# Seven products for w2: 18 of the 22 activation blocks of both FFNs go through nine block pairs, with their activation sums made earlier and kept in DRAM

## The chip, the cores and the metric

The kernel runs on one core of a Trainium2 chip. The time is the device time of one execution in microseconds, as the median of several runs. A profiled execution is a run of its own with its own time; its trace gives the span from the first to the last instruction.

The engines named below: PE is TensorE (matmuls; it writes to PSUM), DVE is VectorE, ACT is ScalarE, POOL is GpSimd, and SP is SyncE, whose queue issues nearly all DMAs in order. "L673" is line 673 of the kernel before; lines of the changed kernel are marked as such.

## The reference

One step of a decoder trunk for 1024 prompt and 32 sample positions, 1056 columns in all, with a model width of 1024. Two FFNs (half steps) enclose a mixer of attention and gated MLP. All is float32:

```python
def swiglu(x, w1, w3, w2):
    return (jax.nn.silu(x @ w1) * (x @ w3)) @ w2          # 1024 -> 2816 -> 1024
...
    h = layer_norm(ALPHA * x + 0.5 * swiglu(x, f1_w1, f1_w3, f1_w2), ln1_g, ln1_b)
    z = h @ w_in + b_in
    ...                                                    # attention, gated MLP: mix
    h = layer_norm(ALPHA * h + mix, ln2_g, ln2_b)
    h = layer_norm(ALPHA * h + 0.5 * swiglu(h, f2_w1, f2_w3, f2_w2), ln3_g, ln3_b)
```

## The kernel before

**Layout.** Activations lie transposed: 128 features on the partitions, the 1056 columns along the free dimension, cut into four chunks of 264 (C). The inner width of an FFN, 2816, is 22 blocks of 128 (f = 0 to 21); the outer width, 1024, is 8 blocks.

**Precision.** Each float32 operand is split into a high and a low part: ACT casts the high part (L213), DVE subtracts it for the low part (L214). A product of 128x128 by 128x264 is then three matmuls, high by high, high by low and low by high (mm3, L202).

**w1 and w3.** For f = 1 to 21, w1 and w3 are one product of 2x2 blocks, done in seven products after Strassen and Winograd rather than eight (hidden). The sums of the activations are made once per FFN (spread, L291 and L301), those of the weights for each f (prep): POOL adds and subtracts (L337 and on), ACT and DVE split. One f takes 7 x 24 = 168 matmuls. Partial products are copied out of PSUM by ACT into buffers M, of which there are six (L397, L399, L400), and joined by DVE (L398, L401, L404, L406, L408). The hidden block, 128x1056, is stored to DRAM (L409).

**w2.** The 22 hidden blocks come back in groups of 2, 4, 6, 6 and 4 (GROUP2). Each loaded block (L614) is split on ACT and DVE. For each of the 8 output blocks and 4 chunks, a group is 3 matmuls per hidden block into one PSUM bank, and DVE adds the bank to the running output Y (L673, the eviction). Nothing here goes by seven products. The last group runs chunk by chunk, with centring (L437 to L448), squares (L487, L491) and normalisation (L497 to L526) of the layer norm between its blocks, and in the first FFN the splits of the next projection's first weights. The sums over columns that the mean needs come from L622 and L624.

**What sets the order.** Generators hold background work in queues (bg, slow, mid); each block ends with a tick that moves them by the number of steps in STEPS or MID. A scheduler then orders each engine's instructions by priority; evictions are urgent. PSUM has three banks tagged mm and five tagged ax. A DMA on SP's queue also waits for the one eight before it. Buffers: 37 slots S of 4 KB (and a little) per partition, eight W for split weights, two R for raw ones, two Q, six M.

## Time and profile before

| | us |
|---|---|
| median of 3 runs | 2258.15 (2256.51 to 2259.08) |
| the profiled execution | 2261.7 |
| its span | 2259.9 |
| first FFN, w1/w3 stage | about 53 to 474 |
| first FFN, w2 stage | 474 to 730 |
| projection, mixer | 730 to 1545 |
| second FFN, w1/w3 stage | 1545 to 1985 |
| second FFN, w2 stage and tail | 1990 to 2260 |

Stages overlap by a few microseconds. Busy time is read for each stage apart, with the engine's share of that stage's length; for PE a missing share is time in which it waited, and the waits name the engine and line that ended them. Some matmul records are missing from a trace, so that counts of a window are a little low.

### The profile page before, as it was taken

How to read it: one execution, taken by the hardware profiler on the slowest of the kernel's cores; microseconds unless marked ns; L12 is line 12 of the kernel's file. 1: busy time of each engine (PE TensorE's matmuls, PEld its weight loads, DVE VectorE, ACT ScalarE, POOL GpSimd, SP SyncE). 2: the span in 40 equal slices, each digit the busy share in tenths (PEclk: the TensorE clock that was granted, in tenths of full speed). 3: DMA queues.
4: the chain of work that ended last, by engine and by line, in shares of the span. 5: the costliest groups of instructions: out<-in, count | busy, mean ns of one | idle time of the engine just before them, and what ended most of it. 6: DMA issues, size and time to landing. Idle time of an engine off the chain costs nothing.

```text
span 2259.9 us, 42304 instructions
## 1 busy us (share of the span) xinstructions
PE 2225.1 (98%) x18031; PEld 2178.4 (96%) x18031; DVE 1185.6 (52%) x2026; ACT 812.2 (36%) x1489; POOL 244.1 (11%) x209
## 2 busy tenths in 40 slices
PE   8999999999999999999999999999999999999997
PEld 7999999999999988888999999999999999999997
DVE  8544344455448417557772624587443344365556
ACT  5333333321114554454463113256333333321114
POOL 3321222000000000000000000012322222000000
PEclk9999999999999999999999999999999999999998
DMA  4222233366324225444532312423332323544311
GB/s 153 95 95 104 95 106 112 123 211 199 134 83 133 108 78 169 126 154 152 182 103 80 108 46 77 175 77 126 120 104 95 113 104 107 208 132 156 100 38 78
DMA packets 81260, 268.61 MB, mean 119 GB/s; under 512 B 15968, under 2 KB 24912, under 8 KB 78384
## 3 DMA queue, kind: packets, MB, share of 16 engines
q1 hardware_dynamic: 80928, 265.86, 35.1%
q8 instruction: 141, 2.31, 0.4%
q14 instruction: 47, 0.39, 0.1%
q10 hardware_dynamic: 144, 0.05, 0.0%
HBM read 224.87 MB, written 87.20 MB: 138 GB/s over the span
## 4 chain that ended last, share of the span: by engine, by line
PE 87%; DVE 5%; DMA 3%; ACT 2%; issue 1%; POOL 0%; SPq 0%; DVEq 0%; ACTq 0%; POOLq 0%
PE mm L202 65%; PE ax L202 19%; DMA S<-kv 1%; PE ax L908 1%; PE ax L933 1%; PE ax L924 1%; DVE X L1087 1%; DVE S L1082 1%; DVE W L214 1%; DMA S<-cD 1%; ACT S L526 1%; DVE S L291 0%; DVE S L214 0%; DMA R<-w13a 0%; DMA S<-xc 0%
## 5 line engine op out<-in xcount | busy, mean ns | idle before, releaser
L202 PE MATMUL mm<-S,W 128*128 128x264 f32 x11040 | 1494.0, 286 | 7.4 <-ACT S L213 3.7
L202 PEld LDWEIGHTS mm<-S,W 128*128 128x128 f32 x11040 | 1401.3, 189 | 23.0 <-issue 7.7
L202 PE MATMUL mm<-S,S 128*128 128x264 f32 x2472 | 388.4, 285 | 5.0 <-POOL Q L337 2.6
L202 PE MATMUL ax<-S,W 128*128 128x264 f32 x2016 | 349.6, 284 | 0.0
L213 ACT CAST W<-R 128x1024 fp32r<-128x1024 f32 (+3 forms) x149 | 145.3, 975 | 553.7 <-PE mm L202 397.1
L202 PEld LDWEIGHTS mm<-S,S 128*128 128x128 f32 x2472 | 336.9, 189 | 6.2 <-POOL Q L337 2.7
L202 PEld LDWEIGHTS ax<-S,W 128*128 128x128 f32 x2016 | 288.1, 188 | 0.0
L202 PE MATMUL ax<-S,S 128*128 128x264 f32 x1512 | 266.0, 286 | 4.3 <-ACT S L213 4.3
L673 DVE SCALAR_TENSOR_TENSOR S<-mm,S 128x264 f32<-128x264 f32 x320 | 135.7, 430 | 198.0 <-PE mm L202 197.2
L214 DVE TENSOR_TENSOR W<-R,W 128x1024 fp32r<-128x1024 f32 (+3 forms) x149 | 169.2, 1136 | 117.8 <-ACT W L213 117.8
L202 PEld LDWEIGHTS ax<-S,S 128*128 128x128 f32 x1512 | 217.8, 189 | 4.7 <-ACT S L213 4.7
L401 DVE TENSOR_TENSOR S<-mm,M 128x264 f32<-128x264 f32 x42 | 18.2, 432 | 247.7 <-PE mm L202 242.8
L337 POOL TENSOR_TENSOR Q<-R 128x512 f32<-128x512 f32 x42 | 60.9, 1450 | 613.7 <-DMA R<-w13b 237.9
L81 POOL CAST S<-ones 128x1 fp32r<-128x1 f32 x32 | 10.1, 343 | 1008.7 <-PE mm L202 937.2
L213 ACT CAST S<-Q 128x1056 fp32r<-128x1056 f32 (+1 forms) x86 | 91.0, 1062 | 48.5 <-DMA Q<-hidA 21.8
L398 DVE TENSOR_TENSOR M<-M,mm 128x264 f32<-128x264 f32 x42 | 18.0, 428 | 169.5 <-PE mm L202 160.2
L214 DVE TENSOR_TENSOR S<-Q,S 128x1056 fp32r<-128x1056 f32 (+1 forms) x86 | 106.0, 1233 | 0.0
L405 ACT ACTIVATE S<-S 128x528 f32<-128x528 f32 x84 | 49.8, 638 | 83.8 <-DVE S L404 83.8
L397 ACT COPY M<-mm 128x264 f32<-128x264 f32 x42 | 15.9, 379 | 157.7 <-PE mm L202 157.7
L811 ACT ACTIVATE S<-mm,cols 128x264 f32<-128x264 f32 (+5 forms) x104 | 46.6, 492 | 65.0 <-PE mm L202 64.8
L912 ACT ACTIVATE M<-M,X 128x128 f32<-128x128 f32 (+1 forms) x96 | 42.7, 446 | 51.4 <-DVE X L909 51.0
L338 POOL TENSOR_TENSOR Q<-Q,R 128x512 f32<-128x512 f32 x42 | 60.1, 1430 | 2.7
(191 smaller groups left out, 1664.8 us busy)
## 6 DMA issues: line engine op xcount, KB each, us to landing
ws<-st SPq DMA_DIRECT2D x144, 256.0 KB
S<-kv SPq DMA_DIRECT2D x48, 512.0 KB
R<-w13b SPq DMA_DIRECT2D x44, 512.0 KB
R<-w13a SPq DMA_DIRECT2D x42, 512.0 KB
R<-wz SPq DMA_DIRECT2D x26, 512.0 KB
Q<-hidA SPq DMA_DIRECT2D x22, 528.0 KB
Q<-hidB SPq DMA_DIRECT2D x22, 528.0 KB
hidA<-S SPq DMA_DIRECT2D x21, 528.0 KB
```

The source lines that it names most:

```text
L202: mm = lambda a, b, s, e: nc.tensor.matmul(o, a[:, cc], b, start=s, stop=e, skip_group_check=True)
L213: self.nc.scalar.copy(hi, src)
L214: self.nc.vector.tensor_tensor(lo, src, hi.bitcast(F32), op=ALU.subtract)
L337: tt(s12[:, lo], cd[:, lo], cd[:, hi], op=ALU.add)
L338: tt(s12[:, hi], s12[:, lo], ab[:, lo], op=ALU.subtract)
L405: lambda x: nc.scalar.activation(h[:, x], h[:, x], AF.Silu),
L526: nc.scalar.activation(y[:, m], y[:, m], AF.Identity, bias=b, scale=g)
L673: nc.vector.scalar_tensor_tensor(y, po, HALF, y, op0=ALU.mult, op1=ALU.add)
L811: put = lambda o, x: nc.scalar.activation(o, x, AF.Identity, bias=b, scale=sc)
L908: nc.tensor.matmul(pS, q[e, i * P : (i + 1) * P], k[e, k0 : k0 + nk], start=True, stop=True)
L912: nc.scalar.activation(s[:, h, :nk], s[:, h, :nk], AF.Exp, bias=ml[:, 0, h, i : i + 1], scale=-1.0, accum_out=ml[:, 1, h, i : i + 1],)
L924: nc.tensor.transpose(pT[:, h, o], s[:, h, o], self.ident)
```

## The change

In both FFNs the hidden blocks 1 to 18 are taken as nine pairs. A pair of hidden blocks (rows), by two chunk pairs (columns), against a pair of output blocks is a 2x2 product of blocks, and it is done by seven products. Blocks 0, 19, 20 and 21 stay plain, 12 matmuls a block and chunk, and come last.

- **Activation sums.** After each even f the w1/w3 stage starts spill_sums for its pair as background work: four differences on DVE, and seven combinations split into high (ACT cast) and low (DVE). The 14 parts of 264 KB are stored to DRAM instead of two hidden blocks of 528 KB. The differences and the high parts use the six buffers M. Hidden blocks are only stored where they are plain.
- **Weight sums.** prep now serves w2 too, at 768 columns: three pairs against one output pair. There its sums are made on DVE, not on POOL; it runs 12 times per FFN.
- **The products.** The nine pairs go in three groups of three. seven does a group against one output pair: 7 products, two chunk pairs each, 9 matmuls for each of these, 126 in all, with an eviction into Y after every product and chunk pair (after: L759). This is done 12 times per FFN.
- **Loads.** 63 loads of 528 KB per FFN bring the sums back, already split (after: L717). For the first group they start in the last f of w1/w3 as its slots come free, mixed with the residual Y (after: L722); for the others they start one output pair before.
- **The end.** Centring starts with the plain blocks and not before them. Its partial means are gathered during the last products (gather). For the first chunk centring and squares come after its sixth block.
- **Others.** The bank pairs of hidden are arranged anew (banks), so two of its three pairs are one kind; MID is 3; the attention tables wait longer between steps.

The diff, cut:

```diff
-GROUP2 = ((2, 4), (4, 2), (6, 1), (6, 1), (4, 2))
+SEVEN = 9
+GP = 3
+NG = SEVEN // GP
+HP = GP * P
+ORDER = (1, 2, 6, 7, 5, 4, 3)
+PLAIN = (0, 19, 20, 21)
+NPL = len(PLAIN)
+NW = 2
+HEAD = 7 * GP + 2 * NC
+AHEAD = 4
...
-STEPS = dict(lead=6, strassen=3, out=2, project=2, gate=1, wout=3)
+STEPS = dict(lead=6, strassen=3, seven=2, out=2, project=2, gate=1, wout=3)
 PAUSE = 6
 REST = 3
-MID = 2
+GAP = 4
+LATE = 16
+MID = 3
...
-    def prep(self, w13, f):
-
-        nc, H = self.nc, KH * P
-        lo, hi = slice(0, H), slice(H, D)
+    def prep(self, src, f, H, engine):
+
+        nc = self.nc
...
-        tt = nc.gpsimd.tensor_tensor
+        tt = engine.tensor_tensor
...
+        else:
+            p4 = []
+            for h, l, w in ((ah, al, D - n), (h12, l12, H - (D - n))):
+                o = H + len(p4) * P
+                self.split(h[:, n : n + w], l[:, n : n + w], cd[:, o : o + w])
+                p4 += part(h, l, n)[: w // P]
...
+    def banks(self):
+        mm, ax = lambda: self.mm_tile()[:, :C], lambda: self.ax_tile()[:, :C]
+        return (ax(), ax()), (mm(), mm()), (mm(), ax())
+
     def hidden(self, f, between):
 
         nc = self.nc
-        bank = lambda: (self.mm_tile()[:, :C], self.ax_tile()[:, :C])
-        one, two, three = bank(), bank(), bank()
+        one, two, three = self.banks()
...
-        nc.sync.dma_start(self.hid[f], h.rearrange("p j h t -> p (j h t)"))
+        if f in PLAIN:
+            nc.sync.dma_start(self.hid[PLAIN.index(f)], h.rearrange("p j h t -> p (j h t)"))
+        elif f % 2:
+            self.odd = h
+        else:
+            self.bg.append(self.spill_sums(f // 2 - 1, self.odd, h))
+
+    def spill_sums(self, i, a, b):
+
+        nc = self.nc
+        x11, x12, x21, x22 = a[:, :, 0], a[:, :, 1], b[:, :, 0], b[:, :, 1]
+
+        def out(p, t):
+            hi = self.M([P, 2, C], F32R)
+            self.split(hi, t.bitcast(F32R), t)
+            dst = self.sums[i, ORDER.index(p)]
+            nc.sync.dma_start(dst[:, 0], hi.bitcast(F32))
+            nc.sync.dma_start(dst[:, 1], t)
+            return self.pause(GAP)
+
+        sub = lambda t, u, v: nc.vector.tensor_tensor(t, u, v, op=ALU.subtract)
+        t1, t2 = (self.M([P, 2, C]) for _ in range(2))
+        sub(t1, x12, x11)
+        yield from out(1, x11)
+        sub(t2, x22, t1)
+        yield from out(5, t1)
+        sub(x12, x22, x12)
+        yield from out(7, x12)
+        t4 = self.M([P, 2, C])
+        sub(t4, x21, t2)
+        yield from out(6, t2)
+        yield from out(3, x22)
+        yield from out(4, t4)
+        yield from out(2, x21)
...
+    def gather(self, c, i, m):
+
+        y = self.Y[c]
+        new = y[i // 2][:, 2 * (i % 2) : 2 * (i % 2) + 2]
+        if i == 1:
+            m = self.M([P, 2, C])
+        if i:
+            self.nc.vector.tensor_tensor(m, y[0][:, :2] if i == 1 else m, new, op=ALU.add)
+        return m
...
+                preps[f] = self.prep(w13[f], f, KH * P, nc.gpsimd)
+            else:
+                preps[f] = self.prep(w2p[f - FB], f, HP, nc.vector)
...
+            if f == FB - 1:
+                load(2)
+            count = iter(range(1, 8))
+
+            def after():
+                between(f, STEPS["strassen"])
+                if f == FB - 1:
+                    load(min(HEAD, 2 + 4 * next(count)))
...
+        self.U = [{p: [] for p in ORDER} for _ in range(NG)]
+        self.Y = [[None, None] for _ in range(NC)]
+        dma = self.nc.sync.dma_start
+
+        def sums(g, p, k):
+            t = self.S([P, 2, 2, C], F32R)
+            dma(t.bitcast(F32), self.sums[g * GP + k, ORDER.index(p)])
+            self.U[g][p].append(t)
+
+        def res(c, k):
+            self.Y[c][k] = self.S([P, KH, C])
+            dma(self.Y[c][k], resid[c, k])
+
+        first = {1: (0, 2), 7: (1, 3)}
+        for g in range(NG):
+            for p in ORDER:
+                for k in range(GP):
+                    yield lambda g=g, p=p, k=k: sums(g, p, k)
+                if g == 0:
+                    for c in first.get(p, ()):
+                        yield lambda c=c: res(c, 0)
+            if g == 0:
+                for c in range(NC):
+                    yield lambda c=c: res(c, 1)
...
+    def seven(self, f, g, np, between):
+
+        nc = self.nc
+        one, two, three = self.banks()
+        y = lambda x, r, e: self.Y[2 * x + e][(2 * np + r) // KH][:, (2 * np + r) % KH]
+        then = {
+            1: (one, 0, 0), 2: (two, 0, 0), 6: (one, 1, 0), 7: (three, 1, 1), 5: (one, 1, 1), 4: (three, 1, 0),
+            3: (one, 0, 1),
+        }
+        for p in ORDER:
+            bank, r, e = then[p]
+            for x in range(2):
+                for k in range(GP):
+                    u = self.U[g][p][k]
+                    self.mm3(
+                        bank[x], *self.L[f][p][k], u[:, 0, x], u[:, 1, x], p in (1, 2, 7) and k == 0, k == GP - 1
+                    )
+                with self.urgent():
+                    nc.vector.scalar_tensor_tensor(
+                        y(x, r, e), bank[x], HALF, y(x, r, e), op0=ALU.mult, op1=ALU.add
+                    )
+            between(p)
...
+                def step(p):
+                    k = ORDER.index(p)
+                    between(f, STEPS["seven"])
+                    if np == KB // 2 - 1:
+                        load(base + min(7 * GP, AHEAD + GP * (k + 1)))
+                    if g == NG - 1 and np == KB // 2 - 2 and k > 4:
+                        fetch(k - 5)
+                    if final:
+                        fetch(k + 2)
+                        if k in (1, 3):
+                            W2.append(next(self.w2units))
+                    if g == NG - 1 and np and 2 <= k < 2 + NC:
+                        means[k - 2] = self.gather(k - 2, np - 1, means[k - 2])
+
+                base = HEAD + 7 * GP * g
+                if np == KB // 2 - 2:
+                    load(base + AHEAD)
+                self.seven(f, g, np, step)
+                del self.L[f]
+                f += 1
...
+        for c in range(NC):
+            self.mid.append(self.center(c, hs, 3 if c else 5, means[c]))
+        centers = list(self.mid)[-NC:]
...
+            for k in range(NPL):
+                hi, lo = H[k]
+                self.mm3(po, w, k * NW * P + n % NW * P, hi[:, cc], lo[:, cc], k == 0, k == NPL - 1)
...
+            early = 6 if c == 0 else 0
+            if mode != "out":
+                self.hold_normed(c)
+                if c == 2:
+                    self.early = [self.unit(self.a["wz"][n], slot=True) for n in range(3)]
+                    self.early = self.early, [self.held([P, NT]) for _ in range(3)]
+            for n in range(KB):
+                if n == early:
+                    self.drain(centers[c])
+                    for m in range(early):
+                        self.square_step(c, m)
+                if c == 0 and n in (1, 3):
+                    W2.append(next(self.w2units))
+                block(n, c)
...
+        w = w2[1 : 1 + 2 * SEVEN].reshape(NG, GP, 2, P, KB // 2, 2, P).transpose(0, 4, 5, 3, 2, 1, 6)
+        A[f"w2p{s}"] = w[:, :, ::-1].reshape(NG * KB // 2, 2, P, 2 * HP)
```

How the instructions lie now, at three places. The names are tile names: M, S, W, R, Q are the buffers above, mm and ax PSUM banks, the numbers running.

ACT in the w1/w3 stage of the first FFN, before, with what each instruction waits for (DMAHW is a DMA lane, the loads and stores of SP's queue):

```order
L397 COPY M_3161<-ax_3156 128x264 [waits PE_49]
L213 CAST W_3375<-R_3369 128x1024 [waits DMAHW0_49,PE_49]
L399 COPY M_3162<-mm_3155 128x264 [waits PE_49]
L399 COPY M_3162<-ax_3156 128x264 [waits PE_49]
L400 COPY M_3163<-mm_3159 128x264 [waits PE_49]
L400 COPY M_3163<-ax_3160 128x264 [waits PE_49]
```

The same place of the changed kernel:

```order
L419 COPY M_3360<-ax_3354 128x264 [waits DMAHW7_49,PE_49,Activation_49]
L419 COPY M_3360<-ax_3355 128x264 [waits PE_49]
L224 CAST M_3396<-S_2875 128x528 [waits DMAHW2_49,Activation_49]
L224 CAST W_3610<-R_3604 128x1024 [waits DMAHW4_49,PE_49]
L224 CAST M_3434<-M_3393 128x528 [waits DVE_49,Activation_49]
L421 COPY M_3361<-ax_3354 128x264 [waits PE_49]
L421 COPY M_3361<-ax_3355 128x264 [waits PE_49]
L224 CAST M_3470<-S_2875 128x528 [waits DMAHW0_49,DVE_49,Activation_49]
L422 COPY M_3362<-mm_3358 128x264 [waits DMAHW2_49,DVE_49,PE_49]
```

Three casts of the sums now lie between the copies out of PSUM, and the first copy into a buffer M also waits for a DMA lane, that is for a store out of that buffer.

SP at the entry into the first FFN's w2 stage, before (L232 the residual, L614 hidden blocks):

```order
L232 DMA S_4963<-xc 128x1056
L614 DMA Q_5278<-hidA 128x1056
L409 DMA hidA<-S_4732 128x1056
L232 DMA S_4965<-xc 128x1056
L232 DMA S_4967<-xc 128x1056
L232 DMA S_4969<-xc 128x1056
```

And in the changed kernel:

```order
L340 DMA R_5581<-w2pa 128x768
L717 DMA S_5308<-sumsA 128x1056
L717 DMA S_5310<-sumsA 128x1056
L341 DMA R_5582<-w2pa 128x768
L196 DMA ws<-st 16x4096
L717 DMA S_5351<-sumsA 128x1056
L196 DMA ws<-st 16x4096
L722 DMA S_5353<-xc 128x1056
L722 DMA S_5355<-xc 128x1056
L432 DMA hidA<-S_5088 128x1056
L717 DMA S_5357<-sumsA 128x1056
```

The loads of sums stand ahead of the last hidden stores, between the raw weights of the first output pairs and the state copies (ws).

DVE at the crowded end of the first FFN's w2 stage, before (L448 centring, L214 splits, L437 and L438 means):

```order
L448 TENSOR_TENSOR S_4965<-S_4965,ax_7525 128x1056
L448 TENSOR_TENSOR S_4973<-S_4973,ax_7525 128x1056
L214 TENSOR_TENSOR S_7889<-R_7887,S_7888 128x1024
L673 SCALAR_TENSOR_TENSOR S_4963<-mm_7612,S_4963 128x264
L437 TENSOR_TENSOR M_7628<-S_4967 128x528
L673 SCALAR_TENSOR_TENSOR S_4971<-mm_7635,S_4971 128x264
L214 TENSOR_TENSOR S_7896<-R_7894,S_7895 128x1024
```

And in the changed kernel, where the last output pair begins (L759 evictions, L494 means, L225 splits, L348 and L349 weight sums, L792 the sum over columns):

```order
L225 TENSOR_TENSOR W_7507<-R_7500,W_7506 128x768
L494 TENSOR_TENSOR M_7616<-S_5468 128x528
L494 TENSOR_TENSOR M_7638<-S_5355 128x528
L348 TENSOR_TENSOR Q_7536<-R_7501 128x384
L494 TENSOR_TENSOR M_7662<-S_5470 128x528
L759 SCALAR_TENSOR_TENSOR S_5576<-ax_7511,S_5576 128x264
L225 TENSOR_TENSOR W_7507<-R_7501,W_7506 128x256
L759 SCALAR_TENSOR_TENSOR S_5546<-mm_7512,S_5546 128x264
L225 TENSOR_TENSOR S_7433<-Q_7381,S_7432 128x768
L792 SCALAR_TENSOR_TENSOR S_7178<-S_7257,X_7136,S_7178 128x1056
```

The weight sums, the means and the sum over columns share DVE with the evictions of the products; centring and squares follow in the plain blocks.

More of the change, by code (lines that the diff above doesn't have):

```diff
@@ L591, in ffn, with ready, between, load @@
         self.Y = self.A = None
-        for f in range(1, FB):
+        loads = deque(self.load_sums(resid))
+        total = len(loads)
+        def ready(f):
             for _ in preps.pop(f):
                 pass
-            if f + 1 < FB:
+            if f < last:
                 begin(f + 1)
-            else:
-                self.begin_out(w2, resid)
-            def between():
-                if f + 1 in preps:
-                    next(preps[f + 1], None)
-                self.tick(STEPS["strassen"])
-            self.hidden(f, between)
+        def between(f, bg):
+            if f + 1 in preps:
+                next(preps[f + 1], None)
+            self.tick(bg)
+        def load(n):
+            with self.tc.high_priority(offset=URGENT):
+                while loads and total - len(loads) < n:
+                    loads.popleft()()
+        for f in range(1, FB):
+            ready(f)
+            if f == FB - 1:
[5 more added lines that the diff above has]
+                    load(min(HEAD, 2 + 4 * next(count)))
+            self.hidden(f, after)
             del self.L[f]
-        self.T, self.L = ({}, {}), {}
+        self.T = ({}, {})
         self.normed = [None] * NC
-        self.out(w2, i, mode)
+        self.out(w2, i, mode, ready, between, load)
     def load_hidden(self, f):
@@ new lines, in out, with fetch, plain_sums, block @@
+    def out(self, w2, i, mode, ready, between, load):
+        nc = self.nc
+        f = FB
+        self.w2units, self.spare = self.units2(w2), False
+        sums = self.column_sums(w2, NPL)
+        H, W2, means = [], [], [None] * NC
+        hs = None
+        raws = deque()
+        def fetch(k):
+            if k < NPL:
+                raws.append(self.load_hidden(k))
+            if k > 0 and len(H) < NPL:
+                with self.fenced():
+                    H.append(self.split_hidden(raws.popleft()))
+        def plain_sums():
+            nonlocal hs
+            hs = self.S([P, NT])
+            for k in range(NPL):
+                raw, w = self.S([P, NT]), self.wsum[:, k : k + 1]
+                nc.sync.dma_start(raw, self.hid[k])
+                yield from self.pause()
+                if k == 0:
+                    nc.vector.tensor_scalar(hs, raw, w, None, op0=ALU.mult)
+                else:
+                    nc.vector.scalar_tensor_tensor(hs, raw, w, hs, op0=ALU.mult, op1=ALU.add)
+                yield
+        for g in range(NG):
+            for np in range(KB // 2):
+                final = g == NG - 1 and np == KB // 2 - 1
+                if g == NG - 2 and np == 0 and mode != "out":
+                    self.bg.append(self.tables())
+                if g == NG - 2 and np == 2:
+                    self.bg.append(sums)
+                if g == NG - 1 and np == 0:
+                    self.drain(sums)
+                    sums = plain_sums()
+                    self.bg.append(sums)
+                if final:
+                    self.drain(sums)
+                ready(f)
+                def step(p):
[5 more added lines that the diff above has]
+                        fetch(k - 5)
+                    if final:
+                        fetch(k + 2)
[9 more added lines that the diff above has]
+                f += 1
+        self.U = self.L = None
+        for c in range(NC):
+            self.mid.append(self.center(c, hs, 3 if c else 5, means[c]))
+        centers = list(self.mid)[-NC:]
+        self.spare = True
+        self.T, self.L = ({}, {}), {}
+        def block(n, c):
+            w = W2[n // NW]
+            po = self.mm_tile()[:, :C]
+            cc = slice(c * C, c * C + C)
+            for k in range(NPL):
+                hi, lo = H[k]
+                self.mm3(po, w, k * NW * P + n % NW * P, hi[:, cc], lo[:, cc], k == 0, k == NPL - 1)
+            y = self.Y[c][n // KH][:, n % KH]
+            with self.urgent():
+                nc.vector.scalar_tensor_tensor(y, po, HALF, y, op0=ALU.mult, op1=ALU.add)
+        for c in range(NC):
+            early = 6 if c == 0 else 0
[12 more added lines that the diff above has]
+                block(n, c)
+                if n >= early:
@@ L745, in tables @@
         nc.sync.dma_start(mk, a["mkP"].partition_broadcast(4))
+        oh = [self.M([NBUCKET, 384]) for _ in range(3)]
         for g in range(3):
-            oh = self.M([NBUCKET, 384])
-            nc.sync.dma_start(oh, a["ohP"][:, g])
-            yield from self.pause()
+            nc.sync.dma_start(oh[g], a["ohP"][:, g])
+        yield from self.pause(LATE)
+        for g in range(3):
             p = self.ax_tile()[:4, :384]
-            nc.tensor.matmul(p, rel[:, 4 * g : 4 * g + 4], oh, start=True, stop=True)
+            nc.tensor.matmul(p, rel[:, 4 * g : 4 * g + 4], oh[g], start=True, stop=True)
             v = self.M([4, 384])
```

183 lines of the change are left out of this document (43 added, 140 removed).

## The prediction

> **What bounds the kernel now.** I read the page's summary and busy shares first, then the table of windows by stage, then what the tensor engine (PE) waits for, then the timelines of the two crowded ends. PE is busy for 98% of the span, and the chain of waits that ends last runs over PE for 87%:
>
> ```profile
> span 2259.9 us, 42304 instructions
> PE 2225.1 (98%) x18031; PEld 2178.4 (96%) x18031; DVE 1185.6 (52%) x2026; ACT 812.2 (36%) x1489; POOL 244.1 (11%) x209
> PE 87%; DVE 5%; DMA 3%; ACT 2%; issue 1%; POOL 0%; SPq 0%; DVEq 0%; ACTq 0%; POOLq 0%
> ```
>
> An average can hide a stage with another limit, so here are the stages: w1/w3 of the first FFN, its w2 stage up to and in the last group, then the same three of the second FFN.
>
> ```profile
> core 0: us, PE busy (x) PEld busy (x) DVE busy (x) ACT busy (x) POOL busy (x), PEclk, DMA share, GB/s
> 55.00:472.00 417.00, 417.00 (x3410) 417.00 (x3410) 176.22 (x291) 145.18 (x248) 99.63 (x76) 1.00 0.33 116
> 472.00:672.00 200.00, 199.52 (x1609) 195.12 (x1608) 104.95 (x187) 34.56 (x37) 0.72 (x4) 1.00 0.43 140
> 672.00:745.00 73.00, 69.60 (x558) 68.25 (x557) 59.87 (x101) 35.27 (x64) 3.26 (x12) 1.00 0.41 138
> 1563.00:1975.00 412.00, 412.00 (x3392) 412.00 (x3392) 173.25 (x289) 144.90 (x246) 98.55 (x76) 1.00 0.35 121
> 1990.00:2174.00 184.00, 183.52 (x1502) 183.10 (x1502) 94.39 (x161) 33.79 (x36) 0.00 (x0) 1.00 0.36 116
> 2174.00:2230.00 56.00, 56.00 (x457) 55.77 (x456) 42.97 (x79) 19.35 (x38) 0.00 (x0) 1.00 0.11 39
> ```
>
> In all of them PE works without a gap at full clock, but for 3.4 us in the last group of the first FFN (73.00 less 69.60), where VectorE (DVE) is busy for 82%. What PE waits for there (first row) and in the second FFN's w2 (second row) is the eviction of a w2 block:
>
> ```profile
> PE mm L202 <- DVE S L673: 3.4, 5, 1.4
> PE mm L202 <- DVE S L673: 0.5, 1, 0.5
> ```
>
> So matmuls removed here come off the end one for one, unless something else then ends later.
>
> **What is removed.** A k-block in w2 costs 8 x 4 x 3 = 96 matmuls of 128x264. A pair costs 192, and seven products of it are 7 x 2 x 3 = 42 for each pair of output blocks, 168 in all. Nine pairs take away 9 x 24 = 216 per FFN, 432 altogether. The second FFN's row gives the pitch of one: 412.00 / 3392 = 0.1215 us. 432 x 0.1215 = **52.5 us** of PE time. I count this in full, since these rows show no idle PE from which it could come instead.
>
> **What is added on DVE.** The rows that price it, by shape, with mean ns behind the busy time:
>
> ```profile
> L673 DVE SCALAR_TENSOR_TENSOR S<-mm,S 128x264 f32<-128x264 f32 x320 | 135.7, 430 | 198.0 <-PE mm L202 197.2
> L214 DVE TENSOR_TENSOR W<-R,W 128x1024 fp32r<-128x1024 f32 x104 | 128.1, 1232 | 73.8 <-ACT W L213 73.8
> L214 DVE TENSOR_TENSOR S<-Q,S 128x1056 fp32r<-128x1056 f32 x44 | 55.0, 1249 | 0.0
> L214 DVE TENSOR_TENSOR W<-R,W 128x768 fp32r<-128x768 f32 x40 | 38.2, 954 | 37.6 <-ACT W L213 37.6
> L448 DVE TENSOR_TENSOR S<-S,ax 128x1056 f32<-128x1056 f32 x24 | 29.3, 1247 | 0.4 <-PE ax L445 0.4
> L491 DVE TENSOR_TENSOR M<-M,M 128x528 f32<-128x528 f32 x35 | 25.7, 734 | 3.5 <-ACT M L487 3.3
> L438 DVE TENSOR_TENSOR M<-M,S 128x528 f32<-128x528 f32 x12 | 8.4, 702 | 0.1
> L624 DVE SCALAR_TENSOR_TENSOR S<-Q,X,S 128x1056 f32<-128x1056 f32 x6 | 7.8, 1308 | 0.0
> ```
>
> In a dense stretch each instruction starts about 0.08 us before the one ahead of it has ended by its own duration (683.72 + 0.70 is 684.42, the next starts at 684.34; and so on down):
>
> ```profile
> 683.72 0.70 DVE L438 TENSOR_TENSOR M<-M,S 128x528 f32<-128x528 f32 x1
> 684.34 1.22 DVE L214 TENSOR_TENSOR W<-R,W 128x1024 fp32r<-128x1024 f32 x1
> 685.48 0.70 DVE L440 TENSOR_TENSOR M<-M,S 128x528 f32<-128x528 f32 x1
> 686.10 0.43 DVE L673 SCALAR_TENSOR_TENSOR S<-mm,S 128x264 f32<-128x264 f32 x1
> 686.44 0.42 DVE L441 TENSOR_TENSOR M<-M 128x264 f32<-128x264 f32 x1
> ```
>
> So I charge duration less 0.08 where DVE is full. [...]
>
> *w1/w3 stage.* A pair adds 11 DVE instructions of 528 (4 differences, 7 low halves): 11 x 0.70 = 7.7 us, and 7 ACT casts of 528 at about 0.63 us (row L405 below), 4.4 us. A pair spans two f, that is 336 matmuls or 40.8 us. DVE goes from 42% (176.22 of 417.00) to 61%, ACT from 35% to 46%. Both stay under PE. Stores add 14 x 0.270 MB less two hidden stores of 0.541 MB: 2.7 MB in 40.8 us, 66 GB/s onto 116. One row shows that the queues can move 424 GB/s (the start of the present w2 stage, where residuals and the first hidden blocks arrive):
>
> ```profile
> 460.00:470.00 10.00, 10.00 (x85) 10.00 (x84) 2.92 (x6) 2.86 (x6) 0.00 (x0) 1.00 1.05 424
> 454.50 5.46 SPq L232 DMA_DIRECT2D S<-xc  x7
> L405 ACT ACTIVATE S<-S 128x528 f32<-128x528 f32 x84 | 49.8, 638 | 83.8 <-DVE S L404 83.8
> ```
>
> A store that waits for its split also holds what is queued behind it on SP, the next f's weights first. Whole f are ahead there: POOL, which adds those weights up, now waits 237.9 us for them, and PE waits for nothing of it:
>
> ```profile
> L337 POOL TENSOR_TENSOR Q<-R 128x512 f32<-128x512 f32 x42 | 60.9, 1450 | 613.7 <-DMA R<-w13b 237.9
> ```
>
> I take **+1** for chance collisions with the PSUM evictions. Below it is nothing (PE never waited in this stage), above it the third rival.
>
> *Entry into w2.* Of the sums, 21 loads of 528 KB and 8 residual loads must come between the first slot that w1/w3 frees and the last product of the first output pair. By the listing of PE's instructions these are 343 matmuls apart: 41.7 us. 29 x 0.541 = 15.7 MB take 37.0 us at 424 GB/s, and SP issues one in 5.46 / 7 = 0.78 us (22.6 us in all), so the queues set the pace. One landing adds 4.4 us (row below), the next weights and the state copies issued there, some 2.6 MB, 6.2 us. That makes 47.6 against 41.7: 0 to 6 us late for each FFN. I take 2, since the loads are issued in the order of use: **+4** for both.
>
> *Inside the sevens.* The next group's 21 loads (11.4 MB, 26.8 us at 424 GB/s) are issued over the 277 matmuls, 33.7 us, before their use: hidden. The evictions per PE time rise: each product of 2 x 9 matmuls (2.19 us) has two evictions, 0.86 us, and the sums of the w2 weights move from POOL to DVE (4 of 384 elements between 0.43 and 0.70 us, splits of 768, 768, 768, 256, 128 about 3.5 us; 5.8 us per 15.3 us of products). DVE: 6.0 + 5.8 of 15.3 us, 77%. A bank isn't asked for again until another product has passed. Waits of 0.28 us, the shortest that the last group shows below, at each of 24 output pairs would be 6.7; at none, 0. I take half, **+3**.
>
> *Start of the plain blocks.* Four hidden blocks are loaded and split late; 4 x 1.249 us of DVE per FFN is the most if nothing covers it, 5.0; products of the last output pair should cover most of it. **+2** for both, ends 0 and 10.
>
> *The crowded end.* This is the largest term. In the listing, DVE's rows from the last output pair of the first FFN to the end of its plain stage hold 150 instructions: 61 evictions (26.2 us), 11 other 264s (5.2), 23 of 528 (16.4), 11 splits of 1024 (13.6), 20 of 1056 (25.0), 4 hidden-sum steps (4.7), 4 splits of 768 (3.8), 4 of 384 and the rest (3.5): 98.4 us by durations, 86.4 less 0.08 each. PE has 662 matmuls there, 80.4 us. DVE is therefore 6.0 us behind at the end, where it now costs 3.4:
>
> ```profile
> 699.38 3.17 PE L202 MATMUL mm<-S,S 128*128 128x264 f32 x24 [0.28 <-DVE S L673]
> 728.29 3.16 PE L202 MATMUL mm<-S,S 128*128 128x264 f32 x24 [0.80 <-DVE S L673]
> 737.97 1.72 PE L202 MATMUL mm<-S,W 128*128 128x264 f32 x12 [1.44 <-DVE S L673]
> 688.03 4.39 DMA R<-w2a
> ```
>
> The bounds are 0 and 98.4 - 80.4 - 3.4 = 14.6. The difference at pitch prices is 2.6; it is a mean over the stretch, and bursts come on top, so I take **+4**. In the second FFN no next projection's weights are split. With each DVE row placed behind the matmul whose bank it reads and the same durations, DVE's lag behind PE peaks there at 3.5 us at pitch prices and 10.8 by durations, where 0.5 is waited now: **+2.5**, ends 0 and 10.3.
>
> **The sum.** -52.5 + 1 + 4 + 3 + 2 + 4 + 2.5 = -36.0. The profiled execution took 2261.7 us, 1.8 beyond its span, and the runs' median is 2258.15, 3.5 below it. 2261.7 - 36.0 = 2225.7 for a profiled execution, **2222** for the runs.
>
> **The rivals.**
>
> *DVE pays whole durations.* Then the ends cost 14.6 + 10.3 = 24.9 in place of 6.5: 18.4 more, 2240.6. For it: PE already waits for DVE there. Against it: the early starts above. 15 in 100.
>
> *Nothing new is waited for.* All added terms are zero: 2258.2 - 52.5 = 2205.7; with one or two small ones up to 2213. For it: PE at 417.00 of 417.00 shows deep buffers. 13 in 100.
>
> *The copies out of PSUM wait for the stores of the sums: slower than before.* The six buffers M hold a w1/w3 stage's partial products and now also ten sums of a pair, and the listing has ACT's first copy of an f wait on a DMA lane. ACT works in order; behind the copy stand the casts and SiLU, and PE soon wants the bank. The copy may be late by two products, 5.84 us, and the idle time of its bank, one product (2.92): 8.8. A lone transfer takes 4.39. Once landing takes 8.8 + 2.0 = 10.8 us the loss over 18 pairs, 36 us, eats the net gain; at 12 us it is 18 x 3.2 = 58, 2280. Against it: 182 of 424 GB/s leaves room. 7 in 100.
>
> *The entry is fed more slowly.* [...] In general: should the queues give a fifth less than 424 when stores and loads mix, the same three parts take 46.3, 7.8 and 4.4 us, and each entry is late by 17 and not by 2: 30 more, 2252, still faster by 6. 4 in 100.
>
> That the products are not really fewer can be left out: the listing has 16608 where 17040 stood.
>
> **How the numbers follow.** My forecast, from 2214 to 2232, has 60 in 100; with 15, 13, 7 and 4 for the rivals 1 is left for anything else. From 2207 to 2243 holds the forecast, nearly all of the first rival and about half of the second. A difference of 0.2%, 4.5 us, is about what measuring this kernel can tell from none. Faster by more: 60 + 15 + 13 + 3 = 91, less 1 for a first rival that also meets other costs: 0.90. Slower: 6 of the third's 7, and 1 of the rest: 0.07. Same: 0.03.
>
> **What would show it.** Matmul rows of 128x264 sum to 16608. In the w1/w3 stages PE stays without idle time and DVE is near 61%; a wait of PE for an ACT copy there means the third rival. At the first products of w2, PE waits for a DMA into a slot by 2 us or so, not 17. In the last 80 us of the first w2 stage PE's waits for evictions sum to 7 us or so; 18 means the first rival, 3 the second. If PE waits inside the sevens by more than 7 us in both FFNs together, a bank or the weight sums on DVE set the pace, and my sum has missed it.

## The result, and the profile after

The changed kernel takes 2217.64 us (median; 2215.42 to 2223.78), the kernel before beside it 2258.13 us. The ratio is 0.9826, with a 95% interval of 0.9805 to 0.9846; measured once more in a later series it was 0.9815 (0.9799 to 0.9831). That is 40.5 us less, where 36 were forecast. Three executions of a later series that took 3062, 3262 and 11,990 us are left out of its ratios.

The summary and the rows of the 128x264 matmuls of the changed kernel (line, engine, names, shapes, count; busy us, mean ns; idle time ahead and what ended most of it):

```profile
span 2215.9 us, 43018 instructions
PE 2175.8 (98%) x17599; PEld 2126.6 (96%) x17599; DVE 1463.6 (66%) x2440; ACT 873.4 (39%) x1655; POOL 288.9 (13%) x209
L213 PE MATMUL mm<-S,W 128*128 128x264 f32 x7224 | 943.5, 287 | 11.1 <-DVE S L846 5.9
L213 PE MATMUL ax<-S,W 128*128 128x264 f32 x4536 | 596.8, 285 | 2.9 <-ACT M L421 2.8
L213 PE MATMUL ax<-S,S 128*128 128x264 f32 x2664 | 391.6, 285 | 1.1 <-ACT S L224 1.1
L213 PE MATMUL mm<-S,S 128*128 128x264 f32 x2184 | 334.9, 287 | 6.8 <-POOL Q L348 2.3
```

The counts sum to 16608, 432 fewer. The span fell by 44.0 us, PE's busy time by 49.3. By stages (w1/w3, sevens and plain blocks of the first FFN, then sevens and plain blocks of the second; columns as in the windows of before; cut at round times, while the sevens end at about 663 and 2146 us):

```profile
55.00:470.00 415.00, 415.00 (x3401) 415.00 (x3401) 288.05 (x401) 175.21 (x312) 121.99 (x76) 1.00 0.51 175
470.00:640.00 170.00, 170.00 (x1364) 165.72 (x1363) 117.24 (x256) 29.39 (x49) 0.00 (x0) 1.00 0.82 304
640.00:730.00 90.00, 82.57 (x655) 80.05 (x653) 79.29 (x141) 43.22 (x75) 6.72 (x19) 1.00 0.48 166
1933.00:2130.00 197.00, 196.93 (x1616) 196.71 (x1615) 133.95 (x288) 39.52 (x67) 0.00 (x0) 1.00 0.73 279
2130.00:2190.00 60.00, 57.50 (x447) 56.20 (x447) 50.59 (x93) 22.58 (x44) 0.00 (x0) 0.97 0.20 70
```

PE still works without a gap in the w1/w3 stage, although DVE's share there rose from 42% to 69% (in the second FFN it shows no wait from 1560 to 1930 us), and in the sevens, although the DMA engines are busy for 82%. In these stages it waits only where the plain blocks begin and after. What it waits for there, the first FFN (470 to 740 us) and then the second (1965 to 2220, without the last layer norm):

```profile
PE mm L213 <- DVE S L846: 5.7, 6, 2.1
PE ax L510 <- DVE M L507: 0.8, 1, 0.8
PE mm L213 <- DVE S L225: 0.7, 1, 0.7
PE mm L213 <- ACT S L224: 0.2, 1, 0.2
...
PE mm L213 <- DVE S L846: 2.3, 2, 2.0
PE mm L213 <- DVE S L225: 0.2, 1, 0.2
```

That is 7.4 us where 3.8 were waited (up to 750 us there, since its last eviction comes at 747), and 2.5 where it was 0.5: 5.6 us more. The granted clock of 0.97 in the last row is new as well.

### The profile page after: what moved, and what is told of

The parts are those of the page before. It is cut to its first block, busy times and chain, and to the rows that moved or that the text cites. A ratio compares the mean times of both kernels' runs of the same rounds, so it can differ in the third digit from the quotient of the medians.

```text
span 2215.9 us, 43018 instructions
## 1 busy us (share of the span) xinstructions
PE 2175.8 (98%) x17599; PEld 2126.6 (96%) x17599; DVE 1463.6 (66%) x2440; ACT 873.4 (39%) x1655; POOL 288.9 (13%) x209
## 4 chain that ended last, share of the span: by engine, by line
PE 86%; DVE 6%; DMA 4%; ACT 2%; issue 1%; POOL 0%; SPq 0%; DVEq 0%; ACTq 0%; POOLq 0%
PE mm L213 44%; PE ax L213 38%; DMA S<-kv 1%; PE ax L1041 1%; PE ax L1066 1%; DVE S L225 1%; PE ax L1057 1%; DMA S<-cD 1%; ACT S L591 1%; DVE S L302 1%; DVE X L1220 0%; DVE S L584 0%; ACT S L224 0%; DVE W L225 0%; DMA S<-xc 0%
## 5 line engine op out<-in xcount | busy, mean ns | idle before, releaser
L213 PE MATMUL mm<-S,W 128*128 128x264 f32 x7224 | 943.5, 287 | 11.1 <-DVE S L846 5.9
L213 PEld LDWEIGHTS mm<-S,W 128*128 128x128 f32 x7224 | 901.4, 189 | 25.9 <-issue 7.8
L213 PE MATMUL ax<-S,W 128*128 128x264 f32 x4536 | 596.8, 285 | 2.9 <-ACT M L421 2.8
L213 PEld LDWEIGHTS ax<-S,W 128*128 128x128 f32 x4536 | 570.7, 188 | 4.3 <-ACT M L421 3.0
L213 PE MATMUL ax<-S,S 128*128 128x264 f32 x2664 | 391.6, 285 | 1.1 <-ACT S L224 1.1
L213 PEld LDWEIGHTS ax<-S,S 128*128 128x128 f32 x2664 | 351.9, 189 | 2.3 <-ACT S L224 1.3
L224 ACT CAST W<-R 128x1024 fp32r<-128x1024 f32 (+4 forms) x177 | 139.9, 807 | 393.1 <-PE mm L213 178.5
L225 DVE TENSOR_TENSOR W<-R,W 128x1024 fp32r<-128x1024 f32 (+4 forms) x177 | 163.3, 928 | 97.9 <-ACT W L224 97.9
L759 DVE SCALAR_TENSOR_TENSOR S<-ax,S 128x264 f32<-128x264 f32 x240 | 99.1, 428 | 60.2 <-PE ax L213 59.9
L348 POOL TENSOR_TENSOR Q<-R 128x512 f32<-128x512 f32 x42 | 64.8, 1542 | 554.7 <-DMA R<-w13b 208.9
L225 DVE TENSOR_TENSOR S<-Q,S 128x1024 fp32r<-128x1024 f32 (+2 forms) x74 | 110.1, 1488 | 7.1 <-ACT S L224 6.4
L225 DVE TENSOR_TENSOR S<-S,M 128x528 fp32r<-128x528 f32 x72 | 84.3, 1171 | 3.6 <-ACT M L224 2.1
L225 DVE TENSOR_TENSOR W<-Q,W 128x1024 fp32r<-128x1024 f32 (+1 forms) x66 | 75.4, 1142 | 8.3 <-ACT W L224 8.3
L349 POOL TENSOR_TENSOR Q<-Q,R 128x512 f32<-128x512 f32 x42 | 74.4, 1771 | 2.7
```

Source lines behind the costliest of these rows:

```text
L213: mm = lambda a, b, s, e: nc.tensor.matmul(o, a[:, cc], b, start=s, stop=e, skip_group_check=True)
L224: self.nc.scalar.copy(hi, src)
L225: self.nc.vector.tensor_tensor(lo, src, hi.bitcast(F32), op=ALU.subtract)
L348: tt(s12[:, lo], cd[:, lo], cd[:, hi], op=ALU.add)
L349: tt(s12[:, hi], s12[:, lo], ab[:, lo], op=ALU.subtract)
L759: nc.vector.scalar_tensor_tensor(y(x, r, e), bank[x], HALF, y(x, r, e), op0=ALU.mult, op1=ALU.add)
```

## The experiments

Medians are compared through the kernel before on the same chip. The kernel before takes 2260.71 to 2261.03 us there. The changed kernel, at 0.982 of it (the mean of 0.9826 and 0.9815), stands for about 2220 us. It has two traces: that of the result, called the first here, and that of the later run.

### One FFN at a time

```diff
-        self.ffn(a["w13b"], a["w2pb"], a["w2b"], 2, "out", self.hD[1])
...
+        self.ffn_o(a["w13b"], a["w2ob"], 2, "out", self.hD[1])
```

ffn_o and what it calls are the methods of the kernel before; with them a flag brings back its bank pairs, its MID and its pauses.

> Only the first FFN is changed, the second is computed as before. Theory (PE sets the end everywhere, what is lost is lost at the crowded end of each FFN): half of the matmuls, 216 x 0.1215 = 26.2 us, less the longer eviction waits of the first FFN (7.4 after, 3.8 before: 3.6) and the 2.8 us wait for an ACT copy at the start of the first w1/w3 stage, if that comes with the new bank pairs: -20 to -23. Rival (the gain comes unevenly, say because the first FFN's crowded end eats most of it): -12 or less here and -28 or more with the second FFN alone.

> Only the second FFN is changed, the first is computed as before. Theory: -26.2 + 2 (eviction waits 2.5 after, 0.5 before), -22 to -25, and together with the first FFN alone the whole of what both bring (-40.5 by the medians). Rival (uneven): -28 or more here, -12 or less with the first alone.

The second of the two has the same edit for the first FFN. Measured: 2240.32 us with the first FFN alone, a ratio of 0.9911 (0.9896 to 0.9926), 20.7 us less; 2241.27 us with the second alone, 0.991 (0.9893 to 0.9926), 19.7 less. Together 40.4, which is what both bring at once: the gain is additive and even, and the uneven rival falls. The second is 2 us short of what I expected; the interval, 16.7 to 24.2 us, covers both.

### Fewer matmuls in the plain blocks, fewer in the sevens

```diff
-                self.mm3(po, w, k * NW * P + n % NW * P, hi[:, cc], lo[:, cc], k == 0, k == NPL - 1)
+                self.mm2(po, w, k * NW * P + n % NW * P, hi[:, cc], lo[:, cc], k == 0, k == NPL - 1)
...
-                    self.mm3(
+                    (self.mm2 if p in (4, 3) else self.mm3)(
```

The first line is one kernel, the second the other; mm2 is mm3 without its last matmul.

> Left out: the third of the three matmuls (low weights by high activations) in the four plain blocks of both FFNs, 256 matmuls, worth 31.1 us at 0.1215 us. Theory (DVE sets the end of the plain stage in the first FFN): there 15.6 us less of PE meet a DVE that already keeps PE waiting, so nearly nothing is gained, 0 to 4; in the second FFN, where DVE is busy for 50.6 of 60 us, 8 to 13. Sum -8 to -17 against the changed kernel, and PE's waits for the evictions grow by the rest. Rival (PE sets the end in the plain stage, the 7.4 us of waits are chance): -26 to -31.

> Left out: the third of the three matmuls in two of the seven products (the fourth and the third) of every output pair of both FFNs, 288 matmuls, worth 35.0 us at 0.1215 us. Theory (inside the sevens PE alone sets the time; DVE 77%, loads hidden): -32 to -35 against the changed kernel. Rival (the loads or DVE's weight sums already pace the sevens without a wait in the record): -17 or less.

Without 256 matmuls in the plain blocks: 2213.16 us, 7 us less of 31. Without 288 in the sevens: 2194.14 us, 26 less of 35. So the plain stage isn't bound by PE alone, as the theory had it, and the gain is even a little under its range. In the sevens the expected 32 to 35 were not reached either. Their traces say what took the rest. Two stretches of the kernel without the 256 (plain stage of each FFN), and a window of 4 us in the first:

```profile
655.00:735.00 80.00, 65.88 (x471) 61.88 (x470) 67.19 (x120) 41.41 (x78) 4.66 (x15) 0.94 0.43 151
2130.00:2200.00 70.00, 57.60 (x431) 55.21 (x430) 61.99 (x116) 33.96 (x67) 0.00 (x0) 0.95 0.26 96
...
679.00:683.00 4.00, 4.00 (x18) 4.00 (x19) 4.00 (x6) 1.39 (x5) 0.00 (x0) 0.50 0.65 197
```

PE waits for 14 and 12 us of these stretches (the second ends in the last layer norm), where the changed kernel waits for 7.4 and 2.5. Behind a wait it worked at half its clock there (0.50 in the last row): 18 matmuls in 4 us, all of it busy, where 34 is usual. The kernel without the 288 shows the same at the last group of the sevens, where PE now overtakes the splits of the weights (PE's timeline):

```profile
619.64 3.16 PE L213 MATMUL ax<-S,W 128*128 128x264 f32 x14 [3.26 <-DVE W L233]
```

The windows around that row:

```profile
616.00:620.00 4.00, 0.74 (x7) 0.53 (x6) 4.00 (x11) 0.00 (x0) 0.00 (x0) 1.00 0.05 19
620.00:624.00 4.00, 4.00 (x23) 4.00 (x22) 4.00 (x9) 0.83 (x1) 0.00 (x0) 0.57 0.00 0
```

DVE is busy without a gap around it. The second FFN's last group has the like: a wait of 2.05 us for a cast at 2095.89 us, then 18 matmuls in 4 us. So PE sets the time in the sevens, with little room left in their last group, and a new wait for DVE or ACT can cost twice: here 3.26 us as a wait, and behind it, at a clock of 0.57, 23 matmuls in 4 us where 34 is usual.

### The weight sums back on POOL

```diff
-                preps[f] = self.prep(w2p[f - FB], f, HP, nc.vector)
+                preps[f] = self.prep(w2p[f - FB], f, HP, nc.gpsimd)
```

> One part undone: the sums of the w2 weights are made on POOL again, not on DVE. It takes 4 x 0.55 = 2.2 us of DVE off each output pair, 53 us in all. Theory (inside the sevens PE never waits, so DVE's load there costs nothing; only the last output pair of an FFN lies in the crowded end): -2 to +1, with the POOL instructions slowing what DVE runs beside them, as they do in the w1/w3 stage, where a DVE subtraction of 528 takes 0.70 us alone and up to 1.7 us beside POOL. Rival (DVE's added load paces the last output pairs): -4 or more.

The changed kernel, run again as the base of this run and the two under the next heading:

> The changed kernel once more, so that the next three are compared with it on one chip. Expected: a ratio to the kernel before of 0.980 to 0.985.

It took 2219.67 us, 0.9815 (0.9799 to 0.9831). With the sums on POOL: 2214.8 us, 0.9792 (0.9777 to 0.9807), 4.9 less, and so the rival's size, not mine. But the trace has no such gain in the sevens: the last eviction of a product in the second FFN comes at the same time in both (2146.3 us in the changed kernel's first trace, 2146.1 here). In its second trace it comes at 2149.5, but from the second FFN's first such eviction to the last all three take 187 us. What is gone is one wait just behind it, and in the first trace the slow clock after that. Here is that place in the changed kernel's first trace, in the timelines of SP, ACT, DVE and PE in turn (start, duration, instruction, and in brackets the idle time ahead of it):

```profile
2133.22 3.05 SPq L203 DMA_DIRECT2D R<-w2b  x2
2137.78 1.83 SPq L701 DMA_DIRECT2D Q<-hidB  x2
...
2144.03 1.08 ACT L224 CAST S<-Q 128x1056 fp32r<-128x1056 f32 x1 [1.23 <-DMA Q<-hidB]
...
2145.15 1.26 DVE L225 TENSOR_TENSOR S<-Q,S 128x1056 fp32r<-128x1056 f32 x1 [0.71 <-ACT S L224]
...
2146.66 2.35 DVE L225 TENSOR_TENSOR S<-R,S 128x1024 fp32r<-128x1024 f32 x2
2148.93 0.43 DVE L846 SCALAR_TENSOR_TENSOR S<-mm,S 128x264 f32<-128x264 f32 x1
...
2149.41 3.01 PE L213 MATMUL mm<-S,W 128*128 128x264 f32 x12 [1.95 <-DVE S L846]
```

And PE at the same place in its second trace:

```profile
2152.61 1.74 PE L213 MATMUL mm<-S,W 128*128 128x264 f32 x12 [1.96 <-DVE S L846]
```

The wait is the same, the slow clock is not: the twelve matmuls take 1.74 us. From the last eviction of a product to the end of the span the two traces take 69.6 and 67.9 us, the kernel with the sums on POOL 65.7.

The last plain blocks are loaded late, behind raw weights and into the two buffers Q; their casts and splits are late; DVE has idle time waiting for the cast; and the first eviction of the plain stage stands behind all that in its order. With the sums on POOL the same two loads went out at 2134.29 us and not at 2137.78. So there were two readings, DVE's work or a late load, and the run with slots, below, tells them apart.

### Squares on POOL, and a finer centring

```diff
-            tt(self.sqs[c][0], self.sqs[c][0], sq, op=ALU.add)
+            nc.gpsimd.tensor_tensor(self.sqs[c][0], self.sqs[c][0], sq, op=ALU.add)
...
-        for j in range(2):
-            tt(y[j], y[j], pm.unsqueeze(1).to_broadcast([P, KH, C]), op=ALU.subtract)
+        for j in range(4):
+            v = y[j // 2][:, 2 * (j % 2) : 2 * (j % 2) + 2]
+            tt(v, v, pm.unsqueeze(1).to_broadcast([P, 2, C]), op=ALU.subtract)
             yield
```

Again two kernels.

> The additions of the squares (528 elements, two or three per chunk) go to POOL in all three layer norms. In the first FFN's crowded end that takes 11 x 0.62 = 6.8 us off DVE, which is 6 us behind there. Theory (the sum of DVE's work sets the waits, 7.4 us in the first FFN and 2.5 in the second): those waits fall, -3 to -6 in all, unless POOL beside DVE slows both: 11 POOL additions at 1.4 us or more, each lengthening DVE's subtractions beside it by 0.5 us or more, take it back, and nothing remains. Rival (single long instructions in front of an eviction set the waits, not the sum): -1 to +1 and the same waits at the same places.

> The subtraction of the mean is done in four instructions of 528 a chunk and not two of 1056. DVE's total stays (16 x 0.62 = 9.9 us a FFN in place of 8 x 1.17 = 9.4), but an eviction can go ahead after 0.6 us and not after 1.2 or 2.4. Theory of the sum: 0 to +1. Rival (single long instructions): the longest waits, 2.1 us in the first FFN and 2.0 in the second, fall by half or more, and with them the lowered PE clock behind the one in the second: -1 to -4.

The squares on POOL take 2223.86 us (0.983, 0.9815 to 0.9844), 4 us more than the changed kernel but with overlapping intervals; the finer centring takes 2232.14 us (0.9867, 0.9852 to 0.9881) and is slower. With the squares on POOL the waits of the two crowded ends add up to 6.9 and 3.4 us, at the same places, instead of 7.4 and 2.5 (6.6 and 2.5 in the second trace). But this does not judge the theory of the sum, since little was taken off DVE. From the last eviction of a product to that of a plain block in the first FFN, the changed kernel first:

```profile
666.10:724.70 58.60, 52.02 (x407) 50.14 (x408) 54.58 (x94) 32.79 (x64) 2.57 (x7) 1.00 0.46 159
666.40:726.10 59.70, 53.32 (x406) 51.63 (x407) 52.70 (x83) 32.69 (x64) 19.67 (x18) 0.97 0.44 152
```

DVE is busy for 1.9 us less, where 6.8 were meant to go: a POOL addition took 1.55 us, and DVE's subtractions beside it grew (those of 1024 into slots S from 1.22 to 1.44 us on average). That is what the expectation named as its exception. The rest of the 4 us is nearer the mixer's end, where the waits add up to 6.6 us instead of 4.5, and ACT's next split ends the longest, 4.2 us.

The finer centring met neither expectation. The four pieces were not spread between the evictions; the timeline of DVE in that kernel has them in one row:

```profile
676.06 1.23 DVE L225 TENSOR_TENSOR S<-R,S 128x1024 fp32r<-128x1024 f32 x1 [2.71 <-ACT S L224]
677.20 2.54 DVE L514 TENSOR_TENSOR S<-S,ax 128x528 f32<-128x528 f32 x4
679.66 0.43 DVE L847 SCALAR_TENSOR_TENSOR S<-mm,S 128x264 f32<-128x264 f32 x1
```

PE behind that eviction:

```profile
680.14 7.07 PE L213 MATMUL mm<-S,W 128*128 128x264 f32 x36 [4.33 <-DVE S L847]
```

DVE itself is idle for 2.71 us ahead of this, because the split at its head waits for ACT's cast of a weight; evictions that could run stand behind it. 36 matmuls then took 7.07 us, where 4.63 is usual. The edit therefore moved DVE's order, not only its grain, and says nothing on grain alone; the rival of single long instructions stays untested.

### Slots for two plain blocks

```diff
-            raw = self.Q([P, NT])
+            raw = self.S([P, NT]) if f >= 2 else self.Q([P, NT])
```

> Of the four plain hidden blocks, the third and fourth are loaded into slots S of their own and no longer wait for the two buffers Q. Nothing else is changed, DVE has the same work. Theory (the waits at the start of the plain blocks come from loads that wait for a buffer, and the eviction stands behind the late splits in DVE's order): the 2.0 us wait in the second FFN goes, and with it the lowered PE clock behind it, about 3.5 us in all, and part of the 1.6 us before 668 us in the first: -3 to -5, a ratio of 0.979 to 0.981 to the kernel before. Rival (DVE's work sets these waits, as the weight sums on POOL could also be read): -1 to +1, 0.981 to 0.983.

> The two changes together: third and fourth plain block in slots of their own, and the weight sums of w2 on POOL. If both only cure the same late loads, this is like either alone, -4 to -6 against the changed kernel, a ratio of 0.979 to 0.980. If DVE's work and the late loads are two causes, the gains add up: -7 to -10, 0.977 to 0.979.

2213.67 us, 0.9793 (0.978 to 0.9807): some 6 us less than the changed kernel, with DVE's work unchanged. What PE waits for in the two crowded ends, the first FFN and then the second, is evictions alone:

```profile
PE mm L213 <- DVE S L846: 4.6, 5, 2.1
...
PE mm L213 <- DVE S L846: 0.6, 2, 0.3
```

In the first FFN that is 4.6 us instead of 7.4 (6.6 in the changed kernel's second trace), in the second 0.6 instead of 2.5. Two windows at the start of the second FFN's plain blocks, in the changed kernel's first trace:

```profile
2146.00:2150.00 4.00, 1.83 (x11) 1.41 (x10) 4.00 (x7) 1.01 (x2) 0.00 (x0) 0.90 0.00 0
2150.00:2154.00 4.00, 4.00 (x25) 4.00 (x25) 1.77 (x5) 0.00 (x0) 0.00 (x0) 0.68 0.00 0
```

The same windows of the kernel with the slots, which is there some 3 us ahead:

```profile
2146.00:2150.00 4.00, 3.67 (x30) 3.55 (x30) 3.13 (x9) 0.00 (x0) 0.00 (x0) 1.00 0.00 0
2150.00:2154.00 4.00, 4.00 (x33) 3.93 (x33) 3.67 (x6) 0.78 (x3) 0.00 (x0) 1.00 0.00 0
```

And its PE at that place:

```profile
2146.45 1.74 PE L213 MATMUL mm<-S,W 128*128 128x264 f32 x12 [0.33 <-DVE S L846]
```

The same twelve matmuls take 1.74 us instead of 3.01; as the second trace of the changed kernel has 1.74 too, only the wait is the slots' doing for certain. From the last eviction of a product to the end this kernel takes 65.6 us, so 2.3 to 4.0 of the 6 us lie there.

Both together, slots and sums on POOL, give 2213.35 us, 0.9788 (0.9776 to 0.9801). The ratio lies in the range given for two causes, the time, 6.7 us less, between the two ranges; but with the slots in place the sums on POOL bring 0.3 us more, where two separate gains would add up to 11. So in the main both cure one thing, the late loads. DVE's sums have a part in what makes them late: in the changed kernel the raw weights ahead of the plain blocks waited 10.6 us in SP's queue for DVE's last weight sum, and the first two plain loads went out at 2128.14 us, with the sums on POOL at 2123.11. The amount of DVE's work as such is not what PE waits for in the second FFN: with the slots it is the same, and the wait is gone. These versions beat both kernels; the one with the slots alone is the smaller edit.

### Stores doubled

```diff
             nc.sync.dma_start(dst[:, 1], t)
+            two = self.twice[i, ORDER.index(p)]
+            nc.sync.dma_start(two[:, 0], hi.bitcast(F32))
+            nc.sync.dma_start(two[:, 1], t)
...
```

> Every part of the activation sums is stored twice, the second time to a place that nothing reads: 3.8 MB more a pair, 93 GB/s on the 175 of the w1/w3 stages, and a buffer M is free only when both have landed. Theory (the copies out of PSUM have slack): PE waits for no copy but the one of 2.8 us at the start, -1 to +4 against the changed kernel. Rival (the slack is nearly used up): PE waits for copies in most pairs, +10 or more.

2220.57 us, 0.9824 (0.9812 to 0.9836): no loss that can be told from none. The first w1/w3 stage of this kernel:

```profile
55.00:470.00 415.00, 415.00 (x3397) 415.00 (x3397) 281.87 (x401) 174.66 (x312) 118.79 (x76) 1.00 0.74 257
```

257 GB/s instead of 175, and PE without a gap. The third rival of the prediction has no ground under it.

### The w1/w3 weight sums on DVE

```diff
-                preps[f] = self.prep(w13[f], f, KH * P, nc.gpsimd)
+                preps[f] = self.prep(w13[f], f, KH * P, nc.vector)
```

> The sums of the w1/w3 weights are made on DVE and not on POOL, four of 512 an f, 4 x 0.69 = 2.8 us more of DVE. Theory (POOL beside DVE slows both, when both work from SBUF to SBUF): DVE's subtractions of 528 for the sums fall from 1.17 and 1.02 us to 0.70, those of 1024 from 1.84 to 1.23, and DVE's busy share in the stage stays near 69%. Rival (the traffic of the stores slows them): they stay as long, and DVE rises to 80% or more. The time changes by -2 to +4 in both, since PE doesn't wait there.

DVE's subtractions for the activation sums and for one weight in the changed kernel (100 to 450 us, by shape; count, busy us, mean ns):

```profile
L225 DVE TENSOR_TENSOR S<-S,M 128x528 fp32r<-128x528 f32 x34 | 40.1, 1181 | 1.3 <-ACT M L224 0.4
L225 DVE TENSOR_TENSOR S<-Q,S 128x1024 fp32r<-128x1024 f32 x17 | 33.4, 1964 | 0.0
```

The same groups of this kernel:

```profile
L225 DVE TENSOR_TENSOR S<-S,M 128x528 fp32r<-128x528 f32 x34 | 24.0, 707 | 4.4 <-ACT M L224 3.6
L225 DVE TENSOR_TENSOR S<-Q,S 128x1024 fp32r<-128x1024 f32 x17 | 20.8, 1221 | 0.0
```

Every one is back at the duration of an undisturbed one (0.70 and 1.23 us in the kernel before), with as many stores as before (180 GB/s), and DVE is busy for 276 of 415 us, less than with POOL's help. The theory holds: it is POOL, not the traffic. The time, 2214.99 us (0.9792, 0.9777 to 0.9806), fell by 5 us, which I hadn't expected. At the start of the first FFN's plain stage this kernel is 5.8 us ahead of the changed one (657.65 against 663.41 us). Most of that is made in the first 55 us, the changed kernel first:

```profile
0.00:55.00 55.00, 45.90 (x322) 42.15 (x323) 45.51 (x50) 30.64 (x43) 21.02 (x14) 0.95 0.44 157
0.00:55.00 55.00, 49.76 (x363) 46.85 (x364) 47.66 (x62) 32.41 (x47) 0.70 (x6) 1.00 0.45 159
```

41 matmuls more are 5.0 us: PE waits 3.9 us less, 2.8 of them the wait for a copy at 53 us, and its clock is 1.00 and not 0.95. Only 2 us are left at the end of the profiled execution, and there the clock took back some of the gain: in the first FFN's plain blocks it is 0.50 from 675 to 679 us, and 0.83 from 1120 to 1140, where the changed kernel's first trace has 1.00 and 0.91.

## Why the prediction was right

**The matmuls: right.** 52.5 us were counted in full, and the two halves of the change gave 40.4 of the 40.5 that both gave. The profiled spans differ by 44.0: 52.5 less 5.6 of new waits at the starts and in the course of the plain blocks, less 1.1 for the slow clock in the second FFN (9 matmuls too few in 4 us), which leaves 1.8 that I have not placed; slow stretches of the clock elsewhere in either execution are not in this sum. The profiled execution of before was 3.5 above its median, and that of the changed kernel was at its median: the 44.0 and the 40.5 differ by just that. Of the 16.5 us of costs that I had forecast, 8.5 came in the profiled execution. That the total came out within 4.5 us is luck in part: three terms, 8 us together, came to nothing, and the slow clock and the unplaced 1.8 were in no term.

**The w1/w3 stage: right that nothing waits, wrong on DVE's share.** 61% was worked out from undisturbed durations; 69% came, since POOL and DVE slow each other (a subtraction of 528 took 1.18 us with the weight sums on POOL, 0.71 with them on DVE). It lay beside PE's work all the same, and my +1 was 0. The wait of 2.8 us at 53 us is no loss: the kernel before waited 3.4 us there for a split.

**The entry into w2: 0, not +4.** The loads moved 377 and 408 GB/s in two windows around the start of the sevens, close to the 424 I had used:

```profile
470.00:480.00 10.00, 10.00 (x85) 10.00 (x84) 5.04 (x11) 0.83 (x1) 0.00 (x0) 1.00 1.03 377
480.00:490.00 10.00, 10.00 (x85) 10.00 (x84) 4.01 (x9) 1.44 (x3) 0.00 (x0) 1.00 1.03 408
```

PE had no wait. My working summed all traffic against the last product; the products in between need only what they have had in order. That is an argument; no run here varies these loads.

**The sevens: 0, not +3.** No record of a wait. I had DVE at 77%; it was busy for 69% of 470 to 640 us. That this leaves little room at its busiest is seen in the kernel without 288 matmuls, which lost 9 of 35 us and waited 3.3 of them for a weight's split in the last group.

**The plain blocks: the sum right, its parts wrong.** I had +2 for late splits, +4 for DVE's total in the first FFN and +2.5 in the second, 8.5 in all. Waits and clock came to 6.7. That the sum fits is luck, for the late splits, my smallest term there, count for more than 2: slots for two raw blocks took the second FFN's waits from 2.5 to 0.6 us and the first's from 7.4 to 4.6, with the same work on DVE. The step that failed is "DVE is therefore 6.0 us behind": I read a sum of work over a stretch as what sets the waits. A DVE that is behind over the whole stretch has no idle time, but it was idle for 10.7 of the 90 us from 640 to 730, in which PE waited 7.4. What sets about half of the waits, 4.7 of 9.9 us, is a few instructions in DVE's order whose own inputs are late. What sets the 4.6 us that are left in the first FFN with the slots no experiment has shown. The longest, 2.1 us, stands behind two subtractions of the mean, and in the changed kernel's trace the chain goes back from them over a split and a cast to the load of a weight of the next projection, which lands at 674 us: a late load again, but untested.

**The rivals.** DVE by whole durations: no, the waits were 7.4 us in the first FFN and not 18. Nothing new waited for: no, 5.6 us were. The copies behind the stores: no, doubled stores cost nothing. A slower feed: no, 377 and 408 GB/s are 11% and 4% under the 424, not a fifth, and no run shows the fifth.

**What I left out.** A wait of PE can lower its clock after it (to 0.50 from 2150 to 2152 us, behind the wait of 1.95 us), and no term of mine had that.

## What to carry to other kernels

Here PE had nearly no gaps, and 432 matmuls less, 52.5 us at their pitch, took 49.3 us off its busy time and 44.0 off the span. The work added beside them in the first w1/w3 stage, which took DVE from 42% to 69%, cost no wait. Where the plain blocks begin and after, PE waited 5.6 us more, and about half of its 9.9 us there, 4.7, went with evictions that stood in DVE's order behind instructions whose own inputs were late. Ask of the engine that frees PE's banks not only how much work it has, but which instruction in its order waits for a late load: slots for two loads were worth 6 us here, while moving the squares to POOL took 1.9 us off DVE in place of 6.8 and gained nothing. Price work for DVE that runs beside POOL at what it takes there: 1.18 us here for a subtraction of 528, and not 0.71.

## What the runs showed of the hardware

**POOL and DVE slow each other.** In the w1/w3 stage of the changed kernel, a POOL addition and a DVE subtraction that overlap, and the same subtraction alone:

```profile
249.66 1.76 POOL L356 TENSOR_TENSOR Q<-R,Q 128x512 f32<-128x512 f32 x1
250.37 1.61 DVE L225 TENSOR_TENSOR S<-S,M 128x528 fp32r<-128x528 f32 x1
255.57 0.70 DVE L225 TENSOR_TENSOR S<-S,M 128x528 fp32r<-128x528 f32 x1
```

1.61 us beside POOL, 0.70 alone. POOL's addition took 1.76 us beside DVE; the same addition in the kernel before (250.38 us), with DVE idle, took 1.29. Evictions, which read one operand from PSUM, kept their 0.43 us: with the w2 sums on POOL the longest of the 336 in the sevens took 0.44 us.

**A wait of 2 us can halve PE's clock.** After 1.95 us of waiting the next 12 matmuls took 3.01 us in the changed kernel's first trace, at a clock of 0.50 from 2150 to 2152 us; after a wait of 1.96 us at the same place they took 1.74 us in its second trace and 1.75 us in the kernel with doubled stores. With the wait of 2.08 us in the first FFN it is the other way round: the clock stayed at 1.00 in the first trace, and in the second it was 0.73 and 0.84 in the two windows of 4 us from 679 us, where that wait ends. So the same wait can lower the clock in one execution and not in another.
